# Ring tiles and `ones` moved to the weights' address modulo 512 bytes, and the gate's last tile in two halves of tokens

## The chip, the cores and the metric

The kernel runs on one core of a Trainium2 chip. The metric is the device time of one execution, in microseconds (us). Four compute engines work side by side on tiles of 128 partitions: TensorE (PE in the profile; its weight loads have a row of their own, PEld), VectorE (DVE), ScalarE (ACT) and GpSimd (POOL). SyncE (SP) issues the DMAs. Each engine takes its own instructions in order; semaphores tie the engines together.

On-chip memory (SBUF) is addressed by partition and by byte within the partition. "Modulo 512" below is the byte address of a tile within its partition, modulo 512.

## The reference

One decoder layer over 2,048 tokens of width 1,024: two groups of token mixers (a gated delta rule and HGRN2), an output projection, a squared-ReLU MLP of width 4,096, and a per-layer embedding `p` that is projected, normed and gated by a projection of the residual.

```python
hn = rms_norm(h, pre_mix_norm[i])
proj = jnp.einsum('btd,dc->btc', hn, w_in[i]).astype(f32)
...
mix = jnp.concatenate([o_a.reshape(bsz, t_len, GDN_WIDTH),
                       o_b.reshape(bsz, t_len, HGRN_WIDTH)], axis=-1).astype(h.dtype)
mix_out = jnp.einsum('btc,cd->btd', mix, w_out[i])
h = h + rms_norm(mix_out, post_mix_norm[i])

u = jnp.einsum('btd,df->btf', rms_norm(h, pre_mlp_norm[i]), w_mlp_up[i])
y = jnp.einsum('btf,fd->btd', jnp.square(jax.nn.relu(u)), w_mlp_down[i])
h = h + rms_norm(y, post_mlp_norm[i])

e = rms_norm(jnp.einsum('bte,ed->btd', p[i], w_ple_proj[i]), ple_norm[i])
gate = jax.nn.sigmoid(jnp.einsum('btd,de->bte', h, w_ple_gate[i]))
h = h + e * gate
```

## The kernel before

**Layout.** Activations are held transposed: 128 features on the partitions, tokens along the free dimension. The 2,048 tokens are four blocks `q` of 512 (`QT`), which is the width of one PSUM bank in fp32. A product of 1,024 features takes eight blocks `k` of 128.

**Split operands.** Each fp32 operand of a large product is held as two fp32r tiles, a rounded high part and the rest (`split`, L161 to L164). A product is three matmuls for each block `k`: weight high by data high, weight high by data low, weight low by data high (`product`, L1102). The weights are the stationary operand of 128x128, that is 512 bytes in each partition; the data are the moving operand of 128x512, that is 2,048 bytes in each partition.

**Stages.** PE's order is written out by hand (the manual schedule for PE, L304); SP's order is too in the mixers and from the MLP on. The stages follow each other on PE:

- *Embedding and mixers:* `mme` (the projection of `p`, L190) and `mm` (the input projection, L1031), 192 and 3,168 matmuls of 512 columns (96 of the latter named `mm_ab`). Between the matmuls of `mm` stand the small fp32 matmuls of the mixers, placed by an agenda that counts matmuls (`tick` and `half`).
- *Output projection:* `mmo`, 768 matmuls.
- *MLP,* for two halves of the tokens, each with an up part `u` of 1,344 and a down part `d` of 1,344 matmuls. Both use Strassen's seven products in place of eight, so VectorE makes sums and differences of blocks between them. In the first block of the up part (weights `w_u`) the last five products are interleaved: three matmuls into one bank, then three into the next.
- *Gate:* `mmg`, 768 matmuls, in two halves; in each, for eight output blocks `d`, the two blocks of tokens follow each other. After a product ACT takes a tanh (L1690), DVE does three steps on it (L1691 to L1693), and the result is stored. The stores of a step `d` are kept in `puts` and issued at the start of the next one (L1678), those of the last step at the end (L1698).

**Where tiles lie.** Pools take SBUF in the order in which they are opened, upward from the bottom; `wp` and later `bp` are taken from the top (`side="right"`). A pool's tiles follow each other, and each tile of a ring has a size that is a multiple of 512 bytes, so that all of a ring's tiles share one address modulo 512. The moving tiles of `mm` and `mme` come from the ring `ra` (10 tiles). From the output projection on, `next_pool` hands out moving tiles in turns of 28: ten from `ra`, then 18 from `rb`. `mixT`, `t` and `h2T` are such tiles. In the gate's second half the tiles of block `q` = 2 all lie in `rb`, and those of `q` = 3 all in `ra`. In the down part both operands (`db` moving, `da` stationary) are tiles of one ring, `bp`. The small tiles of the pools `cp` and `sm`, which have odd sizes, decide at which address the rings behind them begin.

The addresses that the build assigns, modulo 512 bytes:

| tiles | used as | before | after |
|---|---|---:|---:|
| `wp`, `bp`: `w`, `w_out`, `wu`, `wg`, `da` | stationary | 480 | 480 |
| `bp`: `db` | moving in `d` | 480 | 480 |
| `ra`: `pT`, `xt`, 10 of 28 turns of `mixT`, `t`, `h2T` | moving | 288 | 480 |
| `rb`: 18 of 28 turns of `mixT`, `t`, `h2T` | moving | 448 | 480 |
| `st`: `hl` (sums of squares in the norms) | moving | 288 | 480 |
| `ones` | stationary with `hl` | 288 | 480 |
| the mixers' own tiles (`m2`, `mp`) | both, small matmuls | 256 | 288 |

The high and low parts of a moving tile lie 2,048 bytes apart and the blocks of a weight tile 512 bytes apart, so these numbers hold for every matmul.

Of the kernel before, what the change touches and what calls it, by code (L numbers as in the profile page):

```python
# [20 lines left out]
P = 128  # L21
T = 2048
D = 1024
KD = D // P
QT = 512
NQ = T // QT
NC = QT // P
# [57 lines left out]
def trunk(ctx, tc, x, xT, pT, vecs, w_in, w_ab, gdn_a_log, gdn_dt_bias, w_out, w_up, w_down,  # L85
          w_ple, w_gate, consts, out):
    nc = tc.nc
    V, S, G, PE = nc.vector, nc.scalar, nc.gpsimd, nc.tensor

    cp = ctx.enter_context(tc.tile_pool(name="cp", bufs=1))  # L90
    ra = ctx.enter_context(tc.tile_pool(name="ra", bufs=10))
    wctx = ctx.enter_context(ExitStack())
    wp = wctx.enter_context(tc.tile_pool(name="wp", bufs=3, side="right"))
    st = ctx.enter_context(tc.tile_pool(name="st", bufs=2))
    sm = ctx.enter_context(tc.tile_pool(name="sm", bufs=3))
    dr = ctx.enter_context(tc.tile_pool(name="dr", bufs=1, space=DRAM))
    pm = ctx.enter_context(tc.tile_pool(name="pm", bufs=2, space=PSUM))
    pp = ctx.enter_context(tc.tile_pool(name="pp", bufs=4, space=PSUM))
# [10 lines left out]
    cm = mixers.enter_context(tc.tile_pool(name="cm", bufs=1))  # L109
    cst = cm.tile([P, N_CONST, P], F32, name="cst")  # L110
    rows = cp.tile([N_ROWS, P], F32, name="rows")
    dec = cp.tile([4, 2], F32, name="dec")
    ident = cst[:, C_IDENT, :]
    negm = cst[:, C_NEG : C_NEG + 2, :]
    unit = cst[:, C_UNIT, :].rearrange("p (g i) -> p g i", i=SB)
    mask = [cst[:, C_MASK + n, : P if n else P // 2] for n in range(len(LEVELS))]

    cols = cp.tile([P, N_ROWS], F32, name="cols")
    ple_w = cp.tile([P, KD], F32, name="ple_w")

    def col(r):
        return cols[:, r : r + 1]


    lg = cols[:, R_LB : R_LB + 4]
    lb = cp.tile([P, 4], F32, name="lb")
    lb1 = cp.tile([P, 4], F32, name="lb1")
    ha = cp.tile([P, 4], F32, name="ha")
    hna = cp.tile([P, 4], F32, name="hna")
    hb = cp.tile([P, 4], F32, name="hb")  # L130
    nexpa = cp.tile([4, 1], F32, name="nexpa")

    def vectors():

# [12 lines left out]
        S.activation(nexpa, dec[:, 0:1], AF.Exp)  # L147
        V.tensor_scalar(nexpa, nexpa, -1.0, None, ALU.mult)

    mhalf = cp.tile([P, NC], F32, name="mhalf")  # L150
    V.memset(mhalf, -0.5)
    one = cm.tile([P, P], F32, name="one")
    ones = cp.tile([P, P], F32R, name="ones")
    V.memset(one, 1.0)
    V.tensor_copy(ones, one)

# [91 lines left out]
    def tok(q):  # L248
        return slice(q * QT, (q + 1) * QT)
# [64 lines left out]
    xin = {}  # L314
# [42 lines left out]
    with ExitStack() as ectx:  # L357
        es = ectx.enter_context(tc.tile_pool(name="es", bufs=1))
        with tc.manual_schedule(engines={mybir.EngineType.SP}):
            ple0 = stage_ple(0, "plea0")  # L360
            praw = [es.tile([P, 2, QT], F32, name=f"praw{q}") for q in range(2)]
            nc.sync.dma_start(praw[0], pT[:, tok(0)].rearrange("(k p) t -> p k t", p=P))
            rows4 = x[tok(0), :].rearrange("(p c) d -> p c d", c=NC)
            xs = es.tile([P, NC, D], F32, name="xs")
            for c in range(0, NC, 2):
                nc.sync.dma_start(xs[:, c : c + 2], rows4[:, c : c + 2])
            nc.sync.dma_start(ident, consts[:, C_IDENT])
            nc.sync.dma_start(rows, vecs)
            nc.sync.dma_start(dec[:, 0:1], gdn_a_log.rearrange("o h -> h o"))
            nc.sync.dma_start(dec[:, 1:2], gdn_dt_bias.rearrange("o h -> h o"))  # L370
            nc.sync.dma_start(praw[1], pT[:, tok(1)].rearrange("(k p) t -> p k t", p=P))
            ple1 = stage_ple(1, "plea1")
            xraw = es.tile([P, KD, QT], F32, name="xraw")
            for k in range(0, KD, 2):
                nc.sync.dma_start(xraw[:, k : k + 2],
                                  xT[k * P : (k + 2) * P, tok(0)].rearrange("(k p) t -> p k t", p=P))
            nc.sync.dma_start(cst[:, C_NEG:], consts[:, C_NEG:])

            ple = [ple0(V), None]
            pts = [[operand(ra, None, f"pT{q}_{k}", raw=praw[q][:, k]) for k in range(2)] for q in range(1)]  # L380
            ss = sm.tile([P, NC], F32, tag="ss", name="ss_x0")
            for c in range(NC):
                S.activation(xs[:, c], xs[:, c], AF.Square, accum_out=ss[:, c : c + 1])
            V.tensor_scalar(ss, ss, 1.0 / D, EPS, ALU.mult, ALU.add)
            rsqrt(ss)
            stores = []
            for d in range(4):
                stores.append(embed_tile(0, d, ple[0], pts[0], accs, es, 6))
                if d == 1:
                    vectors()  # L390
            pts.append([operand(ra, None, f"pT1_{k}", raw=praw[1][:, k]) for k in range(2)])
            ple[1] = ple1(V)
# [12 lines left out]
    with mixers as mctx:  # L405
# [23 lines left out]
        def x_scale(q):  # L429
            ss2 = sm.tile([P, 2, NC], F32, tag="ss2", name=f"ss2_x{q}")  # L430
            rows4 = x[tok(q), :].rearrange("(p c) d -> p c d", c=NC)
            halves, loaded = [(c, a) for c in range(NC) for a in range(2)], []
            for i in range(len(halves) + 1):
                if i < len(halves):
                    c, a = halves[i]
                    t = m2.tile([P, QT], F32, tag="ld", name=f"xs{q}_{c}_{a}", bufs=2)
                    nc.sync.dma_start(t, rows4[:, c, a * QT : (a + 1) * QT])
                    loaded.append(t)
                if i:
                    c, a = halves[i - 1]  # L440
                    t = loaded.pop(0)
                    S.activation(t, t, AF.Square, accum_out=ss2[:, a, c : c + 1])
                yield
            ss = sm.tile([P, NC], F32, tag="ss", name=f"ss_x{q}")
            V.tensor_tensor(ss, ss2[:, 0, :], ss2[:, 1, :], ALU.add)
            V.tensor_scalar(ss, ss, 1.0 / D, EPS, ALU.mult, ALU.add)
            rsqrt(ss)
            yield
            x_r[q] = spread(ss, f"x{q}")
# [828 lines left out]
    prep, x = None, {}  # L1278
# [391 lines left out]
    for half in range(2):  # L1670
        qs = (2 * half, 2 * half + 1)
        if half == 0:
            later(gate_operands(2), range(8, 24, 2))
            later(gate_operands(3), range(32, 48, 2))
        for d in range(KD):
            w = gated.pop((half, d))
            for a in puts:
                nc.sync.dma_start(*a)  # L1678
            puts = []
            if d + 1 == KD and half == 0:  # L1680
                rsb = {q: spread_load(ple_r[q], f"pg{q}", None, "acc", 3) for q in (2, 3)}
            for s, q in enumerate(qs):
                ps = bank(f"mmg_{q}_{d}", pp)
                product(ps, columns(*w), xin[q])
                nq, nd = (q, d + 1) if d + 1 < KD else (q + 2, 0)
                if nq < NQ:
                    es[nq, nd] = embedded(nq, nd, rsb[nq])
                t = es.pop((q, d))
                e, th = t[:, 0], t[:, 1]
                S.activation(th, ps, AF.Tanh, scale=0.5)  # L1690
                V.scalar_tensor_tensor(th, th, 1.0, e, ALU.add, ALU.mult)  # L1691
                V.tensor_tensor(th, th, xin[q][d][:, 0, :], ALU.add)
                V.tensor_tensor(th, th, xin[q][d][:, 1, :], ALU.add)  # L1693
                puts.append((out[blk(d), tok(q)], th))
                if s == 0:
                    gate_weights(half, d + 2)
    for a in puts:
# [46 lines left out]
```

## Time and profile before

| what | us |
|---|---:|
| time, median of 3 runs | 2778.44 |
| lowest and highest of the 3 | 2771.64 and 2778.57 |
| the profiled execution: its span, first to last instruction | 2778.2 |
| PE busy in it | 2696.7 |
| DVE busy | 2048.2 |
| ACT busy | 1471.2 |

The page lists the span of the profiled execution and no further time of its own; the span is 0.2 us below the median of the runs. "Busy" is the union of an engine's instructions. A matmul's row gives the mean length of one from start to end (about 390 to 400 ns), but matmuls overlap: what counts is how far one starts after the other, and that is a stretch of PE's work divided by its count.

The stages on PE, by the first start and the last end of their matmuls in the trace: `mme` and `mm` 7 to 1140 us, `mmo` 1141 to 1337, the first `u` 1336 to about 1662, the first `d` until about 1982, the second `u` until 2286, the second `d` until 2594, `mmg` until 2772.

### The profile page before, as it was taken

The numbers are of one execution on the slowest core, as the hardware profiler recorded it, in microseconds if no ns is written. First come the engines' busy times: TensorE is split into PE (matmuls) and PEld (weight loads), VectorE is DVE, ScalarE is ACT, GpSimd is POOL, SyncE is SP. The second block draws the span as 40 slices with busy tenths as digits, with TensorE's granted clock in tenths as the row PEclk, the third lists the DMA queues.
The fourth block names the chain that finished last, engine by engine and source line by source line (L and its number), as shares of the span: only waits on it lengthen the run. The fifth ranks groups of instructions, "written<-read, shape, count | busy, mean of one in ns | idle before, by whom it ended". The sixth has DMA issues, their size and how long they took to land.

```text
span 2778.2 us, 38362 instructions
## 1 busy us (share of the span) xinstructions
PE 2696.7 (97%) x12721; PEld 2219.1 (80%) x12721; DVE 2048.2 (74%) x4242; ACT 1471.2 (53%) x2943; POOL 104.2 (4%) x104
## 2 busy tenths in 40 slices
PE   7999999999999999999899999999999999999999
PEld 5787788878888887777688887887888888887887
DVE  6787877787787777578889867758787765567775
ACT  6665554455545445676555545545454455465431
POOL 0000000000000000000000000001000000001000
PEclk9999999999999999999999999999999999999999
DMA  7776776667666665887466547667454446577663
GB/s 261 261 242 217 230 249 220 218 215 244 231 211 215 213 213 166 267 300 241 141 222 217 181 149 252 222 192 247 155 197 145 147 165 210 190 254 246 213 207 118
DMA packets 268598, 589.24 MB, mean 212 GB/s; under 512 B 55642, under 2 KB 59960, under 8 KB 249200
## 3 DMA queue, kind: packets, MB, share of 16 engines
q1 hardware_dynamic: 268400, 586.79, 63.2%
q8 instruction: 101, 1.65, 0.2%
q14 instruction: 97, 0.79, 0.1%
HBM read 419.75 MB, written 166.92 MB: 211 GB/s over the span
## 4 chain that ended last, share of the span: by engine, by line
PE 62%; DVE 9%; DMA 8%; issue 6%; ACT 3%; SPq 1%; POOL 1%; DVEq 0%; POOLq 0%; ACTq 0%
PE u L1100 22%; PE d L1100 20%; PE mm L1031 9%; PE mmg L1100 6%; DMA ud_g<-u_g 2%; DMA sys_g<-ud_g 1%; DVE pr_g L667 1%; DVE xs_g L670 1%; DVE xs_g L672 1%; PE mmo L1100 1%; DMA mixT<-mixd 1%; DMA rsb_g<-rd_g 1%; DMA b<-h1d 0%; DMA rd_g<-m_g 0%; DVE acc_vg L511 0%
## 5 line engine op out<-in xcount | busy, mean ns | idle before, releaser
L1031 PE MATMUL mm<-xt,w 128*128 128x512 f32 x3072 | 787.0, 403 | 1.9 <-ACT qk_h L767 0.9
L1031 PEld LDWEIGHTS mm<-xt,w 128*128 128x128 f32 x3072 | 558.6, 190 | 109.7 <-ACT qk_h L767 1.3
L1100 PE MATMUL d<-db,da 128*128 128x512 f32 x2688 | 613.0, 390 | 3.9 <-DVE db L217 1.9
L1100 PE MATMUL u<-t,wu 128*128 128x512 f32 x2604 | 608.0, 396 | 3.3 <-ACT wu L163 3.3
L1100 PEld LDWEIGHTS d<-db,da 128*128 128x128 f32 x2688 | 503.9, 188 | 112.3 <-DVE db L217 4.7
L1100 PEld LDWEIGHTS u<-t,wu 128*128 128x128 f32 x2604 | 489.5, 188 | 121.2 <-ACT wu L163 4.1
L217 DVE TENSOR_TENSOR db<-db 128x512 fp32r<-128x512 f32 x224 | 161.2, 720 | 72.6 <-ACT db L216 71.7
L1429 DVE TENSOR_TENSOR u<-u,u 128x512 f32<-128x512 f32 x224 | 150.3, 682 | 72.5 <-PE u L1100 71.3
L216 ACT ACTIVATE db<-db 128x512 fp32r<-128x512 f32 x224 | 140.9, 629 | 82.2 <-DMA db<-hid 80.2
L1100 PE MATMUL mmo<-mixT,w_out 128*128 128x512 f32 x720 | 172.9, 401 | 7.2 <-DVE w_out L164 5.8
L1100 PE MATMUL mmg<-h2T,wg 128*128 128x512 f32 x768 | 178.1, 394 | 0.0
L1470 ACT ACTIVATE u<-u 128x512 f32<-128x512 f32 x128 | 81.0, 633 | 179.5 <-DVE u L1429 179.0
L1100 PEld LDWEIGHTS mmg<-h2T,wg 128*128 128x128 f32 x768 | 144.3, 188 | 33.5
L1100 PEld LDWEIGHTS mmo<-mixT,w_out 128*128 128x128 f32 x720 | 137.3, 191 | 41.8 <-DVE w_out L164 7.1
L164 DVE TENSOR_TENSOR da<-da 128x512 fp32r<-128x512 f32 x128 | 92.7, 724 | 90.2 <-ACT da L163 89.8
L163 ACT ACTIVATE da<-da 128x512 fp32r<-128x512 f32 x128 | 80.5, 629 | 137.6 <-DMA da<-sumd 113.0
L163 ACT ACTIVATE wu<-a 128x512 fp32r<-128x512 f32 x124 | 74.1, 624 | 47.9 <-DMA a<-in_w_up_dram 45.1
L667 DVE TENSOR_TENSOR pr_g<-xs_g,sys_g 128x16 f32<-128x16 f32 (+14 forms) x240 | 93.8, 391 | 5.4
L227 POOL TENSOR_TENSOR acc_y<-acc_y,sq_y 128x512 f32<-128x512 f32 x28 | 38.4, 1371 | 1393.3 <-ACT sq_y L226 1393.3
L164 DVE TENSOR_TENSOR wu<-a,wu 128x512 fp32r<-128x512 f32 x124 | 84.7, 686 | 4.9 <-ACT wu L163 4.8
L1471 ACT ACTIVATE u<-u 128x512 f32<-128x512 f32 x128 | 80.8, 631 | 3.7
L672 DVE SCALAR_TENSOR_TENSOR xs_g<-xs_g,sys_g 128x4 f32<-128x4 f32 x256 | 57.6, 225 | 29.3 <-DMA sys_g<-ud_g 23.9
(374 smaller groups left out, 3817.6 us busy)
## 6 DMA issues: line engine op xcount, KB each, us to landing
w<-cache_in SPq DMA_DIRECT2D x96, 1024.0 KB
db<-hid SPq DMA_DIRECT2D x224, 256.0 KB
cache_in<-w SPq DMA_DIRECT2D x32, 1024.0 KB
hid<-u SPq DMA_DIRECT2D x128, 256.0 KB
da<-sumd SPq DMA_DIRECT2D x128, 256.0 KB
a<-in_w_up_dram SPq DMA_DIRECT2D x124, 256.0 KB
hid<-ht SPq DMA_DIRECT2D x96, 256.0 KB
dr<-in_w_down_dram SPq DMA_DIRECT2D x96, 256.0 KB
```

What stands on the lines that cost most here:

```text
L163: S.activation(t[:, 0], raw, AF.Copy)
L164: eng.tensor_tensor(t[:, 1], raw, t[:, 0], ALU.subtract)
L216: S.activation(t[:, 0], plain(t), AF.Copy)
L217: V.tensor_tensor(t[:, 1], plain(t), t[:, 0], ALU.subtract)
L227: eng.tensor_tensor(acc, acc, sq, ALU.add)
L667: V.tensor_tensor(pr[:, :, :, 0:i], xs[:, None, :, 0:i].broadcast_to([P, 2, GC, i]), sys[:, 0:i, i : i + 2].rearrange("p j two -> p two j" ...
L672: V.scalar_tensor_tensor(xs[:, :, i + 1], xs[:, :, i], sys[:, i, i + 1 : i + 2], xs[:, :, i + 1], ALU.mult, ALU.add)
L1031: PE.matmul(ps, *terms[i], start=i == 0, stop=i == nt - 1)
L1100: PE.matmul(ps, a, b, start=start, stop=stop)
L1429: V.tensor_tensor(c[new], c[old], ps, ALU.add)
L1470: S.activation(c[k], c[k], AF.Relu)
L1471: S.activation(c[k], c[k], AF.Square)
```

## The change

It does two things.

**Addresses.** Small tiles go into a new pool `c0` ahead of the ring `ra`; `cp` is opened behind `st`, with `ones` as its first tile; a pad of 64 bytes goes into `sm`. With that, `ra`, `st`, `ones` and `rb` begin at 480 modulo 512, as the table shows. The column of scales `ss_x` moves to `c0` with two buffers where it had three.

**The last tile.** For the last block of tokens and the last output block (`q` = 3, `d` = 7) the product is done for the first 256 tokens into one bank and then for the other 256 into a second one; tanh, the three steps on DVE and the store are done for each half.

```diff
-    cp = ctx.enter_context(tc.tile_pool(name="cp", bufs=1))
+    c0 = ctx.enter_context(tc.tile_pool(name="c0", bufs=1))
     ra = ctx.enter_context(tc.tile_pool(name="ra", bufs=10))
     wctx = ctx.enter_context(ExitStack())
     wp = wctx.enter_context(tc.tile_pool(name="wp", bufs=3, side="right"))
     st = ctx.enter_context(tc.tile_pool(name="st", bufs=2))
+    cp = ctx.enter_context(tc.tile_pool(name="cp", bufs=1))
+    ones = cp.tile([P, P], F32R, name="ones")
     sm = ctx.enter_context(tc.tile_pool(name="sm", bufs=3))
+    sm.tile([P, 16], F32, tag="pad", name="pad", bufs=1)
...
-    dec = cp.tile([4, 2], F32, name="dec")
+    dec = c0.tile([4, 2], F32, name="dec")
...
-    ple_w = cp.tile([P, KD], F32, name="ple_w")
+    ple_w = c0.tile([P, KD], F32, name="ple_w")
...
-    lb = cp.tile([P, 4], F32, name="lb")
+    lb = c0.tile([P, 4], F32, name="lb")
...
-    ones = cp.tile([P, P], F32R, name="ones")
...
-            ss = sm.tile([P, NC], F32, tag="ss", name="ss_x0")
+            ss = c0.tile([P, NC], F32, tag="ss", name="ss_x0", bufs=2)
...
             for s, q in enumerate(qs):
-                ps = bank(f"mmg_{q}_{d}", pp)
-                product(ps, columns(*w), xin[q])
+                parts = [slice(0, QT)] if (q, d) != (NQ - 1, KD - 1) else [slice(0, QT // 2), slice(QT // 2, QT)]
+                banks = []
+                for i, at in enumerate(parts):
+                    ps = bank(f"mmg_{q}_{d}_{i}", pp)[:, : at.stop - at.start]
+                    product(ps, columns(*w), [x[:, :, at] for x in xin[q]])
+                    banks.append((at, ps))
...
-                e, th = t[:, 0], t[:, 1]
-                S.activation(th, ps, AF.Tanh, scale=0.5)
-                V.scalar_tensor_tensor(th, th, 1.0, e, ALU.add, ALU.mult)
-                V.tensor_tensor(th, th, xin[q][d][:, 0, :], ALU.add)
-                V.tensor_tensor(th, th, xin[q][d][:, 1, :], ALU.add)
-                puts.append((out[blk(d), tok(q)], th))
+                for at, ps in banks:
+                    e, th = t[:, 0, at], t[:, 1, at]
+                    S.activation(th, ps, AF.Tanh, scale=0.5)
+                    V.scalar_tensor_tensor(th, th, 1.0, e, ALU.add, ALU.mult)
+                    V.tensor_tensor(th, th, xin[q][d][:, 0, at], ALU.add)
+                    V.tensor_tensor(th, th, xin[q][d][:, 1, at], ALU.add)
+                    puts.append((out[blk(d), q * QT + at.start : q * QT + at.stop], th))
```

The order of the instructions on every engine is the same as before up to the last tile of the gate. At the program's end, PE's rows of the last product were these (`mmg` is the bank, `h2T` the moving tiles, `wg` the weights; the size is that of the output):

```order
L1100 MATMUL mmg_7_25963<-h2T_0_25165,wg_7_0_25826 128x512 x3
L1100 MATMUL mmg_7_25963<-h2T_1_25203,wg_7_0_25826 128x512 x3
L1100 MATMUL mmg_7_25963<-h2T_2_25233,wg_7_0_25826 128x512 x3
L1100 MATMUL mmg_7_25963<-h2T_3_25253,wg_7_0_25826 128x512 x3
L1100 MATMUL mmg_7_25963<-h2T_4_25291,wg_7_1_25831 128x512 x3
L1100 MATMUL mmg_7_25963<-h2T_5_25325,wg_7_1_25831 128x512 x3
L1100 MATMUL mmg_7_25963<-h2T_6_25345,wg_7_1_25831 128x512 x3
L1100 MATMUL mmg_7_25963<-h2T_7_25383,wg_7_1_25831 128x512 x3
```

Now there are twice as many of half the width, in two banks; around the turn from the first bank to the second they read:

```order
L1102 MATMUL mmg_7_0_25967<-h2T_5_25329,wg_7_1_25835 128x256 x3
L1102 MATMUL mmg_7_0_25967<-h2T_6_25349,wg_7_1_25835 128x256 x3
L1102 MATMUL mmg_7_0_25967<-h2T_7_25387,wg_7_1_25835 128x256 x3
L1102 MATMUL mmg_7_1_25992<-h2T_0_25169,wg_7_0_25830 128x256 x3
L1102 MATMUL mmg_7_1_25992<-h2T_1_25207,wg_7_0_25830 128x256 x3
L1102 MATMUL mmg_7_1_25992<-h2T_2_25237,wg_7_0_25830 128x256 x3
```

So each weight block is loaded six times in this product where it was loaded three times. On DVE the end of the program was, with `eg` the tile of the embedding and the tanh:

```order
L1691 SCALAR_TENSOR_TENSOR eg_7_25893<-eg_7_25893 128x512
L1692 TENSOR_TENSOR eg_7_25893<-eg_7_25893,h2T_7_25042 128x512
L1693 TENSOR_TENSOR eg_7_25893<-eg_7_25893,h2T_7_25042 128x512
L1691 SCALAR_TENSOR_TENSOR eg_7_25925<-eg_7_25925 128x512
L1692 TENSOR_TENSOR eg_7_25925<-eg_7_25925,h2T_7_25383 128x512
L1693 TENSOR_TENSOR eg_7_25925<-eg_7_25925,h2T_7_25383 128x512
```

and is now:

```order
L1698 SCALAR_TENSOR_TENSOR eg_7_25897<-eg_7_25897 128x512
L1699 TENSOR_TENSOR eg_7_25897<-eg_7_25897,h2T_7_25046 128x512
L1700 TENSOR_TENSOR eg_7_25897<-eg_7_25897,h2T_7_25046 128x512
L1698 SCALAR_TENSOR_TENSOR eg_7_25929<-eg_7_25929 128x256
L1699 TENSOR_TENSOR eg_7_25929<-eg_7_25929,h2T_7_25387 128x256
L1700 TENSOR_TENSOR eg_7_25929<-eg_7_25929,h2T_7_25387 128x256
L1698 SCALAR_TENSOR_TENSOR eg_7_25929<-eg_7_25929 128x256
L1699 TENSOR_TENSOR eg_7_25929<-eg_7_25929,h2T_7_25387 128x256
L1700 TENSOR_TENSOR eg_7_25929<-eg_7_25929,h2T_7_25387 128x256
```

The last three steps were one triple of 512 tokens and became two triples of 256. ACT has one tanh more and SP one store more, in the same manner.

More of the change, by code (lines that the diff above doesn't have):

```diff
@@ L125, in trunk @@
     lg = cols[:, R_LB : R_LB + 4]
-    lb = cp.tile([P, 4], F32, name="lb")
[L127 to L131, printed above, removed]
+    lb = c0.tile([P, 4], F32, name="lb")
+    lb1 = c0.tile([P, 4], F32, name="lb1")
+    ha = c0.tile([P, 4], F32, name="ha")
+    hna = c0.tile([P, 4], F32, name="hna")
+    hb = c0.tile([P, 4], F32, name="hb")
+    nexpa = c0.tile([4, 1], F32, name="nexpa")
     def vectors():
@@ L148, in vectors @@
         V.tensor_scalar(nexpa, nexpa, -1.0, None, ALU.mult)
-    mhalf = cp.tile([P, NC], F32, name="mhalf")
+    mhalf = c0.tile([P, NC], F32, name="mhalf")
     V.memset(mhalf, -0.5)
     one = cm.tile([P, P], F32, name="one")
-    ones = cp.tile([P, P], F32R, name="ones")
     V.memset(one, 1.0)
@@ L443, in x_scale @@
                 yield
-            ss = sm.tile([P, NC], F32, tag="ss", name=f"ss_x{q}")
+            ss = c0.tile([P, NC], F32, tag="ss", name=f"ss_x{q}", bufs=2)
             V.tensor_tensor(ss, ss2[:, 0, :], ss2[:, 1, :], ALU.add)
```

## The prediction

> **What bounds the kernel now.** I read the page from the top: the span, the engines, the chain that ended last and its shares.
>
> ```profile
> span 2778.2 us, 38362 instructions
> PE 2696.7 (97%) x12721; PEld 2219.1 (80%) x12721; DVE 2048.2 (74%) x4242; ACT 1471.2 (53%) x2943; POOL 104.2 (4%) x104
> PE 62%; DVE 9%; DMA 8%; issue 6%; ACT 3%; SPq 1%; POOL 1%; DVEq 0%; POOLq 0%; ACTq 0%
> PE u L1100 22%; PE d L1100 20%; PE mm L1031 9%; PE mmg L1100 6%; DMA ud_g<-u_g 2%; DMA sys_g<-ud_g 1%; DVE pr_g L667 1%; DVE xs_g L670 1%; DVE xs_g L672 1%; PE mmo L1100 1%; DMA mixT<-mixd 1%; DMA rsb_g<-rd_g 1%; DMA b<-h1d 0%; DMA rd_g<-m_g 0%; DVE acc_vg L511 0%
> ```
>
> PE is busy 97% of the span. The chain runs through it in the up part `u`, the down part `d` and the gate `mmg`, and only for a small part in the mixers (`mm`) and the output projection (`mmo`). The change takes no large matmul away, so the question is how far apart matmuls start. The groups give counts and the idle time before them (the last numbers):
>
> ```profile
> L1031 PE MATMUL mm<-xt,w 128*128 128x512 f32 x3072 | 787.0, 403 | 1.9 <-ACT qk_h L767 0.9
> L1100 PE MATMUL d<-db,da 128*128 128x512 f32 x2688 | 613.0, 390 | 3.9 <-DVE db L217 1.9
> L1100 PE MATMUL u<-t,wu 128*128 128x512 f32 x2604 | 608.0, 396 | 3.3 <-ACT wu L163 3.3
> L1100 PE MATMUL mmo<-mixT,w_out 128*128 128x512 f32 x720 | 172.9, 401 | 7.2 <-DVE w_out L164 5.8
> L1100 PE MATMUL mmg<-h2T,wg 128*128 128x512 f32 x768 | 178.1, 394 | 0.0
> ```
>
> All five have the same shapes, yet `d` takes 613.0/2688 = 228 ns for each matmul and `u` 608.0/2604 = 233 ns. The chain in order of time (start, length, what) has long unbroken runs, which give cleaner rates:
>
> ```profile
> 1552.46 107.30 PE u L1100 x460
> 1683.61 193.21 PE d L1100 x851
> 1982.61 303.23 PE u L1100 x1304
> 2299.92 212.61 PE d L1100 x938
> 2603.47 168.56 PE mmg L1100 x728
> ```
>
> That is 233.3, 227.0, 232.5, 226.7 and 231.5 ns. Only in `d` do moving and stationary tiles share their address modulo 512 (480 and 480); in `u` and `mmg` the moving tiles are at 448 or 288. So before already holds both cases. Two rows more rule out the nearest other reasons. `d` turns to another bank after every three matmuls, and so does most of the first block of `u`, which the timeline shows (start, length, count):
>
> ```profile
> 1353.00 10.41 PE L1100 MATMUL u<-t,w_u 128*128 128x512 f32 x44
> ```
>
> Less the 0.40 us that the last one takes, 10.0/43 = 233 ns: turning banks doesn't make a product fast. And the gate's last products differ in the ring alone. The tanh on ACT starts when a product is done:
>
> ```profile
> 2760.95 0.60 ACT L1690 ACTIVATE eg<-mmg 128x512 f32<-128x512 f32 x1 [4.90 <-PE mmg L1100]
> 2766.61 0.60 ACT L1690 ACTIVATE eg<-mmg 128x512 f32<-128x512 f32 x1 [5.07 <-PE mmg L1100]
> 2772.11 0.60 ACT L1690 ACTIVATE eg<-mmg 128x512 f32<-128x512 f32 x1 [4.90 <-PE mmg L1100]
> ```
>
> The 24 matmuls of `q` = 2 (`rb`, 448) took 5.66 us, the 24 of `q` = 3 (`ra`, 288) 5.50 us: same weights, same code, 236 against 229 ns.
>
> The Trainium skill says otherwise: by SBUF — State Buffer, section "Who interferes with whom", PE reads moving data and weights through two independent ports and never waits on anyone. By that rule no address would matter and the change would be worth its tail alone; it is the first rival below. These rows disagree with it.
>
> **The change, part by part.** After it all large matmuls stand as those of `d` do. I take 226.8 ns for them, between the two runs of `d`.
>
> *Up part.* The first block (84 matmuls) lies among waits, so I leave it out; it could add 0.5 us. The first half then has 1260 x (233.3 - 226.8) = 8.2 us, the second 1344 x (232.5 - 226.8) = 7.7 us. What could take the place of PE is DVE, which makes the weights' sums. The windows (PE, PEld, DVE, ACT, POOL busy, clock, DMA) of the two halves:
>
> ```profile
> 1372.00:1660.00 288.00, 287.19 (x1230) 231.51 (x1231) 233.94 (x378) 158.37 (x264) 0.00 (x0) 1.00 0.56 193
> 1983.00:2285.00 302.00, 302.00 (x1301) 244.12 (x1300) 224.61 (x357) 154.34 (x255) 0.00 (x0) 1.00 0.47 161
> ```
>
> DVE works 233.94 of 288 us (81%); against a stage shorter by 8.2 us that is 84%. PE waits for nothing there. I take all of it: **15.9 us**.
>
> *Gate.* 744 x (231.5 - 226.8) = **3.5 us**; PE has no idle time in its row.
>
> *Mixers.* The rate of `mm` from an unbroken run of the chain, and what the chain and the waits say of the stage:
>
> ```profile
> 668.11 3.68 PE mm L1031 x16
> by line: PE mm L1031 28.8%; issue 13.2%; DMA ud_g<-u_g 4.9%; DMA sys_g<-ud_g 4.0%; DVE pr_g L667 3.7%; DVE xs_g L670 2.7%; DVE xs_g L672 2.3%; DMA rsb_g<-rd_g 1.7%; DVE acc_vg L511 1.4%; DVE raw_xt L952 1.3%; DVE xt L164 1.2%; SPq L647 1.2%
> PE psc_g L743 <- ACT w_g L740: 14.4, 15, 4.1
> 100.00:600.00 500.00, 477.62 (x2566) 402.91 (x2565) 391.45 (x1098) 275.85 (x692) 25.39 (x29) 0.99 0.70 230
> 600.00:1100.00 500.00, 492.99 (x2701) 419.63 (x2699) 381.53 (x1117) 259.39 (x688) 27.86 (x32) 1.00 0.64 215
> ```
>
> 3.68/16 = 230.0 ns, so 3.2 ns are to be had 3360 times (`mm`, `mm_ab`, `mme`): 10.8 us. But between 262 and 1140 us the chain spends only 28.8% in `mm`; it goes through round trips of DMA and short DVE steps, and PE waits for the recurrence (`psc_g`) in 15 places. There a faster PE waits longer. On the other side PE is busy 477.62 and 492.99 of 500 us, and much of what those waits hang on was itself released by PE some tens of us earlier. So between 29% (3.1 us) and all (10.8 us); nearer the lower middle: **6.0 us**. The mixers' small matmuls move both operands together from 256 to 288 and keep their distance; I cost that at nothing, and the norms' matmuls, equal at 288 before and at 480 after, too.
>
> *Output projection.* Its moving tiles are split over the rings as the gate's are, so 768 x 4.7 = 3.6 us are to be had. But its chain is elsewhere:
>
> ```profile
> by line: issue 19.0%; PE mmo L1100 9.9%; DMA b<-h1d 6.2%; DVE w_out L164 5.1%; DMA mixT<-mixd 5.0%; DVE t L164 4.0%; DVE acc_o L227 3.1%; ACT L1137 2.9%; DMA raw_out<-in_w_out_dram 2.7%; ACT L1136 2.5%; DVE yo L1170 2.5%; ACT w_out L163 2.4
> ```
>
> 9.9% of it would give 0.4, all of it 3.6; I take **1.0 us**.
>
> *The last tile.* After the last matmul come one tanh, three DVE steps and a store, one behind the other. Rows of before for the full and the half width, for narrow matmuls, and for the store's issue:
>
> ```profile
> 2772.11 0.60 ACT eg L1690
> 2772.74 0.70 DVE eg L1691
> L767 ACT ACTIVATE th_h<-mm x32: 363/381/383, 89.8 to 1067.7; 128x256 f32<-128x256 f32 x32
> L635 DVE TENSOR_TENSOR y_kg<-y_kg,gf_g 128x256 f32<-128x256 f32 x16 | 6.6, 414 | 0.0
> 467.56 0.45 PE at_h L822 x4
> 2774.91 0.33 SPq L1698 DMA_DIRECT2D out_dram<-eg  x1
> ```
>
> For the second half the tanh takes 0.38 in place of 0.60 and each DVE step 0.41 in place of 0.70: 0.22 + 3 x 0.29 = 1.1 us less behind the last matmul. The first half's steps (0.38 + 3 x 0.41 = 1.6 us) lie under the second bank's product. The store runs from 2774.91 to the span's end, 3.3 us, and now carries half the bytes: between 0 and half of that, I take 0.3. Matmuls of 256 columns in this format aren't in the trace. Below, half of 226.8 or the 0.45/4 = 112 ns of narrow matmuls that each load their own weights: 48 x 113 = 5.4 us against 5.5 before. Above, the weight load sets the pace and a half takes as long as a whole: 48 x 226.8 = 10.9 us. The narrow row is the nearest, so 0.1 us less. Sum **1.5 us**, with ends at 4.0 lost and 2.8 gained.
>
> *The rest.* `ss_x` with two buffers: each is used once per block of tokens, hundreds of us apart, so nothing waits.
>
> Sum: 15.9 + 3.5 + 6.0 + 1.0 + 1.5 = 27.9 us. Span 2778.2 - 27.9 = 2750.3; the median lies 0.2 above the span: **2750.5 us**.
>
> **Rivals.**
> *The address is not the reason* (6%). Then `d` is faster because its two operands come from one ring, or were written just before use, and only the tail is left: 2778.4 - 1.5 = 2777. For it: no other stage has equal addresses in a long run. Against it: 233 ns with turning banks, and 236 against 229 ns for two rings in one code.
>
> *Another engine takes over* (6%). If DVE, at 81%, holds the first half of `u`, and mixers and output projection give nothing, 8.2 + 6.0 + 1.0 are lost: 2766. Against it: no wait for DVE in `u` behind its first block.
>
> *The clock falls where PE waits* (3%), the one that ends slower. In the mixers one wait of 4 us was followed by slow matmuls (timeline, then windows with the clock behind POOL):
>
> ```profile
> 431.09 0.80 PE L743 MATMUL psc_g<-w_g,kt_g 128*128 128x128 f32 x2 [4.06 <-ACT w_g L740]
> 433.67 3.31 PE L1031 MATMUL mm<-xt,w 128*128 128x512 f32 x8
> 424.00:432.00 8.00, 3.94 (x22) 3.21 (x21) 7.31 (x28) 5.42 (x14) 0.00 (x0) 0.84 1.02 387
> 432.00:440.00 8.00, 8.00 (x39) 7.02 (x39) 6.81 (x22) 1.60 (x3) 1.01 (x1) 0.73 0.48 172
> ```
>
> Eight matmuls took 3.31 us, 414 ns each, and at clocks of 0.84 and 0.73 the 16 us lost 8 x 0.16 + 8 x 0.27 = 3.4 us. If all 15 waits at `psc_g` grew to 4 us, that would cost 15 x 3.4 = 51 us: 2802. It decides from a wait of about 4 us on; but a head's share of `mm`, some 200 matmuls, saves 0.6 us, and the mean wait is 14.4/15 = 1.0 us. The Trainium skill gives the same point in TensorE: Matmul & The Clock Gate, Part 1 (half rate after an idle window of about 3.4 us); the wait of 4.06 us agrees.
>
> **How the numbers follow.** The forecast has 85%. Its low end takes everything: 15.9 + 0.5 + 3.5 + 10.8 + 3.6 + 2.8 = 37.1, so 2741; runs of before also lie up to 6.8 us under their median, so 2738. Its high end takes 3.1 from the mixers, nothing from the output projection and the dear tail: 15.9 + 3.5 + 3.1 - 4.0 = 18.5, so 2760; a part of the second rival brings 2763. A difference of 0.3% (8.3 us) is about what a measurement of this kernel can tell. Forecast and second rival are faster by more (90%), the first lies within (7%), the third is slower (3%).
>
> **What would show it.** In the profile after: runs of `u` and `mmg` on the chain at 226 to 228 ns for each matmul, `u` and `mmg` as fast as `d`, and `d` unchanged; `mm` at 227 in unbroken runs, with `psc_g` waits grown by a few us in total; behind the last matmul one tanh of 0.38 and three steps of 0.41 us. The prediction is wrong if `u` stays at 233 ns, if a wait for DVE appears in `u`, or if the matmuls of 256 columns start over 200 ns apart.

## The result, and the profile after

The changed kernel takes 2758.36 us (median of 4 runs, 2755.88 to 2764.09) against 2777.82 us for the one before (4 runs, 2771.64 to 2778.57). The ratio is **0.993**, with a 95% interval of 0.991 to 0.994: 19.5 us faster, where 27.9 were forecast. The profiled execution took 2759.13 us, 1.8 us more than its span.

From the page of the changed kernel: the span, the busy times, and the five groups of large matmuls (count, then busy time and mean ns of one, then idle time of PE ahead of them):

```profile
span 2757.3 us, 38414 instructions
PE 2673.0 (97%) x12745; PEld 2221.0 (81%) x12745; DVE 2046.0 (74%) x4245; ACT 1469.8 (53%) x2944; POOL 104.2 (4%) x104
L1033 PE MATMUL mm<-xt,w 128*128 128x512 f32 x3072 | 785.5, 402 | 1.3 <-ACT zt_zg L548 0.7
L1102 PE MATMUL d<-db,da 128*128 128x512 f32 x2688 | 613.5, 390 | 5.8 <-DVE db L219 3.2
L1102 PE MATMUL u<-t,wu 128*128 128x512 f32 x2604 | 593.3, 390 | 3.5 <-ACT wu L165 3.4
L1102 PE MATMUL mmo<-mixT,w_out 128*128 128x512 f32 x720 | 170.5, 398 | 9.7 <-DVE w_out L166 6.2
L1102 PE MATMUL mmg<-h2T,wg 128*128 128x512 f32 (+1 forms) x792 | 174.7, 383 | 0.0
```

PE has 24 instructions more (the halves) and is busy 23.7 us less; the other engines do what they did. `u` lost 14.7 us, `d` nothing, and `mm`, which has the most matmuls, only 1.5 us. The unbroken runs on the chain that ended last (start, length) give the rates:

```profile
1368.60 80.69 PE u L1102 x348
1449.75 94.29 PE u L1102 x416
1544.49 104.28 PE u L1102 x460
1673.28 207.69 PE d L1102 x915
1972.87 295.60 PE u L1102 x1304
2587.03 165.36 PE mmg L1102 x752
```

The second `u` run went from 232.5 to 295.60/1304 = 226.7 ns for each matmul, the rate of `d` (207.69/915 = 227.0). Of the first half's runs two are as fast (94.29/416 and 104.28/460 = 226.7), the first is not: 80.69/348 = 231.9.

The weight loads are not what became shorter. Their group in `u`, before and then after, has the same length, 188 ns for each load; what fell, by 14.7 us, is the idle time between the loads:

```profile
L1100 PEld LDWEIGHTS u<-t,wu 128*128 128x128 f32 x2604 | 489.5, 188 | 121.2 <-ACT wu L163 4.1 <-DVE wu L164 0.9
L1102 PEld LDWEIGHTS u<-t,wu 128*128 128x128 f32 x2604 | 489.6, 188 | 106.5 <-ACT wu L165 4.2 <-DVE wu L166 0.7
```

Cut at the first matmul of each stage, the two executions compare so (lengths taken before rounding):

| stage | starts, before | starts, after | length before | after | difference |
|---|---:|---:|---:|---:|---:|
| work ahead of `mm_ab` | 0 | 0 | 44.8 | 45.3 | +0.5 |
| mixers | 44.8 | 45.3 | 1096.1 | 1090.8 | -5.2 |
| `mmo` | 1140.8 | 1136.2 | 195.6 | 195.6 | 0.0 |
| first `u` | 1336.4 | 1331.7 | 326.0 | 319.6 | -6.4 |
| first `d` | 1662.4 | 1651.3 | 310.0 | 311.3 | +1.3 |
| second `u` | 1972.4 | 1962.6 | 313.3 | 305.7 | -7.6 |
| second `d` | 2285.7 | 2268.3 | 307.9 | 308.8 | +0.9 |
| `mmg` | 2593.5 | 2577.1 | 178.5 | 175.3 | -3.2 |
| behind the last matmul | 2772.0 | 2752.4 | 6.1 | 4.9 | -1.2 |
| span | | | 2778.2 | 2757.3 | -20.9 |

The output projection is the stage in which PE became faster and nothing was won. Its windows, before and then after (length, then busy time of PE, PEld, DVE, ACT, POOL with counts, granted clock, DMA share, GB/s):

```profile
1140.84:1336.43 195.59, 188.21 (x799) 150.63 (x798) 142.08 (x211) 122.81 (x192) 3.02 (x3) 0.98 0.79 265
```

```profile
1136.16:1331.73 195.57, 185.87 (x800) 151.52 (x798) 141.99 (x211) 122.28 (x192) 3.02 (x3) 0.97 0.78 265
```

PE is busy 2.3 us less in a stage of the same length: the time turned into waiting, as the group's idle time says too (7.2 before, 9.7 now, most of it for `w_out`). The end of the program on ACT (tanh, with PE's product ahead of it in brackets) and on DVE:

```profile
2741.22 0.60 ACT L1697 ACTIVATE eg<-mmg 128x512 f32<-128x512 f32 x1 [4.84 <-PE mmg L1102]
2746.72 0.60 ACT L1697 ACTIVATE eg<-mmg 128x512 f32<-128x512 f32 x1 [4.90 <-PE mmg L1102]
2749.59 0.39 ACT L1697 ACTIVATE eg<-mmg 128x256 f32<-128x256 f32 x1 [2.27 <-PE mmg L1102]
2752.41 0.38 ACT L1697 ACTIVATE eg<-mmg 128x256 f32<-128x256 f32 x1 [2.43 <-PE mmg L1102]
...
2752.82 0.43 DVE L1698 SCALAR_TENSOR_TENSOR eg<-eg 128x256 f32<-128x256 f32 x1 [1.47 <-ACT eg L1697]
2753.28 0.43 DVE L1699 TENSOR_TENSOR eg<-eg,h2T 128x256 f32<-128x256 f32 x1
2753.74 0.42 DVE L1700 TENSOR_TENSOR eg<-eg,h2T 128x256 f32<-128x256 f32 x1
```

The halves' products ended 2.87 and 2.82 us after the tanh ahead of them, so the 48 matmuls of 256 columns start (2.87 + 2.82)/48 = 119 ns apart.

### The profile page after: what moved, and what is told of

Same layout as the page of the kernel before. It is cut to its first block, busy times and chain, and to the rows that moved or that the text cites. A ratio compares the mean times of both kernels' runs of the same rounds, so it can differ in the third digit from the quotient of the medians.

```text
span 2757.3 us, 38414 instructions
## 1 busy us (share of the span) xinstructions
PE 2673.0 (97%) x12745; PEld 2221.0 (81%) x12745; DVE 2046.0 (74%) x4245; ACT 1469.8 (53%) x2944; POOL 104.2 (4%) x104
## 4 chain that ended last, share of the span: by engine, by line
PE 63%; DVE 10%; DMA 8%; issue 5%; ACT 4%; SPq 1%; POOL 1%; DVEq 0%; POOLq 0%; ACTq 0%
PE u L1102 21%; PE d L1102 19%; PE mm L1033 11%; PE mmg L1102 6%; DMA ud_g<-u_g 1%; DMA sys_g<-ud_g 1%; PE mmo L1102 1%; DVE pr_g L669 1%; DVE xs_g L672 1%; DMA raw_out<-in_w_out_dram 1%; DVE xs_g L674 1%; DVE raw_xt L954 1%; DMA db<-hid 1%; DVE xt L166 1%; DMA b<-h1d 1%
## 5 line engine op out<-in xcount | busy, mean ns | idle before, releaser
L1102 PE MATMUL u<-t,wu 128*128 128x512 f32 x2604 | 593.3, 390 | 3.5 <-ACT wu L165 3.4
L1102 PE MATMUL mmg<-h2T,wg 128*128 128x512 f32 (+1 forms) x792 | 174.7, 383 | 0.0
L166 DVE TENSOR_TENSOR da<-dr,da 128x512 fp32r<-128x512 f32 x96 | 66.3, 690 | 17.6 <-ACT da L165 15.4
```

Source lines behind the costliest of these rows:

```text
L166: eng.tensor_tensor(t[:, 1], raw, t[:, 0], ALU.subtract)
L1102: PE.matmul(ps, a, b, start=start, stop=stop)
```

## The experiments

What was forecast is the address theory: a large matmul starts 226.7 ns after the one before it where its two operands have the same address modulo 512, and 4 to 7 ns later otherwise. Three questions were put: is it the address, and of which ring; what is the period and how does the price depend on the distance; and why did the mixers not become as fast.

### 1 and 2: the two halves of the change, each alone

Addresses alone, the changed kernel without the halves:

```diff
-                parts = [slice(0, QT)] if (q, d) != (NQ - 1, KD - 1) else [slice(0, QT // 2), slice(QT // 2, QT)]
+                parts = [slice(0, QT)]
```

> The addresses of the change, the gate's last tile whole as before. Theory (the equal address modulo 512 gives nearly all of the gain): 2758.4 + 1.2 = about 2760 us, u and mmg at 226 to 227 ns for each matmul. Rival (the last tile in halves matters): clearly above 2765.

Measured: 2760.83 us (2758.49 to 2765.39), ratio 0.994 [0.992, 0.995]. The second `u` run took 295.58 us for its 1304 matmuls, as after.

The halves alone, in the kernel before:

```diff
-                ps = bank(f"mmg_{q}_{d}", pp)
-                product(ps, columns(*w), xin[q])
+                parts = [slice(0, QT)] if (q, d) != (NQ - 1, KD - 1) else [slice(0, QT // 2), slice(QT // 2, QT)]
+                banks = []
+                for i, at in enumerate(parts):
...
```

> The addresses of before, the gate's last tile in two halves. Theory: only the tail changes, some 1.2 us less than before (2777.8): 2776 to 2777, and on the chain u stays at 232 to 234 ns, mmg at 231 to 232. The mixers end where they ended before (the first mmo starts at 1140.8 us), within a us. Rival (the mixers' end wanders from build to build by some us whatever the addresses): the first mmo starts 3 us or more away from 1140.8.

Measured: 2778.18 us (2776.56 to 2782.11), ratio 1.000 [0.999, 1.001]. `u` ran as before (303.23/1304 = 232.5 ns), and behind the last matmul stood 4.9 us in place of 6.1. So the gain belongs to the addresses. The tail's 1.2 us are seen in the trace but not in the time, whose interval of 0.1% either way (2.8 us) is wider than that. One thing missed the theory and nearly reached the rival's 3 us: although nothing changed ahead of the gate, the mixers ended 2.8 us earlier than before. The first block of `mmo` in this run (count, lengths, from when to when):

```profile
L1059 PE MATMUL mmo<-mixT,w_out x48: 388/392/481, 1138.0 to 1151.1; 128*128 128x512 f32 x48
```

Before, it began at 1140.8, after the change at 1136.2. The mixers' length moves by itself; experiment 5 comes back to it.

### 3: one ring at a time

`rb` alone to 480 (`ra` stays at 288), in the kernel before:

```diff
+    sm.tile([P, 8], F32, tag="pad", name="pad", bufs=1)
```

> Before with 32 bytes of padding, so that the ring rb lies at 480 as the weights do and ra stays at 288; last tile whole. rb holds 64% of u's and 56% of mmg's and mmo's moving tiles. Theory: u saves 1728 x 6.7 = 11.6, mmg 432 x 6.7 = 2.9, the mixers nothing: about 2763; the last products of the gate take 5.44 us for q = 2 and still 5.50 for q = 3. Rival (the relation of both rings matters): less than half of that, above 2770.

Measured: 2771.09 us (2766.37 to 2778.51), ratio 0.998 [0.997, 0.999]. The gain is 6.8 us, under half of the change's.

`ra` alone at 480 (`rb` back at 448), in the changed kernel:

```diff
-    sm.tile([P, 16], F32, tag="pad", name="pad", bufs=1)
+    sm.tile([P, 8], F32, tag="pad", name="pad", bufs=1)
```

> After with 32 bytes less of padding: ra and the norms' tiles at 480, rb at 448; last tile in halves. Theory: u saves 960 x 5 = 4.7, mmg 336 x 2.3 = 0.8, the mixers the 4.7 us that they gained in after, the tail 1.2: about 2766. If the mixers' gain is not of the addresses: about 2771, with the first mmo starting near 1140.

Measured: 2774.82 us (2772.55 to 2778.97), ratio 0.999 [0.998, 1.000], a gain of 3.1 us. Both theories missed, and on the same side; with `rb` alone it was the rival's number that came (above 2770). Together they are 6.8 + 3.1 = 9.9 us, with 1.2 us of tail in the second, where both rings together brought 2777.88 - 2760.83 = 17.1 us. **The gains don't add up.** The chain's `u` runs of the two kernels, `rb` alone and then `ra` alone:

```profile
1976.33 300.92 PE u L1101 x1304
```

```profile
1976.60 303.02 PE u L1102 x1304
```

`u` takes 18 of 28 tiles from `rb` and 10 from `ra`, that is 864 and 480 of 1344 matmuls. The steady prices of the addresses of before are 6.6 ns for a tile of `rb` and 2.2 ns for one of `ra` (the table of experiment 4). If each matmul paid for its own tile alone, `rb` in place would have given 864 x 6.6 ns = 5.7 us; the run went from 303.23 to 300.92 us, 2.3 less. `ra` in place should have given 480 x 2.2 ns = 1.1 us and gave 0.2. By the starts of `u`'s matmuls in the trace, those with a tile of `rb` began 230.7 ns after the one ahead of them though they now had the weights' address. The gate, where a whole product takes its tiles from one ring, shows why. With `rb` alone at 480, a product of `rb` follows one of `ra`, and the gaps in it were, by the same starts:

```
behind the 1st to 10th matmul of the product:   224 to 236 ns, up and down
behind the 11th to 24th:                        226.8 ns
```

So a matmul at another address costs not only itself; up to ten matmuls behind it still run unevenly. In `u` the rings change after three to nine matmuls nearly everywhere, and one misplaced ring spoils most of the other's gain. One place in each block of the second `u` has 18 matmuls of `rb` in a row, and there the gaps came to 226.6 to 226.8 ns from the eleventh on. The products of the gate in this run, by the tanh behind each:

```profile
2751.52 0.60 ACT L1691 ACTIVATE eg<-mmg 128x512 f32<-128x512 f32 x1 [4.91 <-PE mmg L1101]
2757.07 0.60 ACT L1691 ACTIVATE eg<-mmg 128x512 f32<-128x512 f32 x1 [4.95 <-PE mmg L1101]
2762.59 0.60 ACT L1691 ACTIVATE eg<-mmg 128x512 f32<-128x512 f32 x1 [4.92 <-PE mmg L1101]
```

The product of `rb` took 5.55 us (5.66 before the change), that of `ra` 5.52 us. The starts of the matmuls are the finer measure (a median over the products of the gate's second half): 5.49 us for `rb` (5.61 before), not the 24 x 226.7 ns = 5.44 of an even run, and 5.51 us for `ra` (5.49 before).

### 4: the distance and the period

Three kernels put the rings at other distances from the weights, by a first tile `shift` in `c0`, the pad in `sm`, and `gcol` taken from `sm` to the mixers' pool `mp`:

```diff
+    c0.tile([P, 64], F32, name="shift")
...
-    sm.tile([P, 16], F32, tag="pad", name="pad", bufs=1)
+    sm.tile([P, 120], F32, tag="pad", name="pad", bufs=1)
...
-            gcol = sm.tile([P, NC, 36], F32, tag="gcol", name=f"gcol_{q}", bufs=2)
+            gcol = mp.tile([P, NC, 36], F32, tag="gcol", name=f"gcol_{q}", bufs=2)
```

This one has `ra` 256 bytes and `rb` 32 bytes away from the weights; `shift` of 16 columns with the old pad gives 64 and -64, 32 columns with a pad of 112 give 128 and -128.

> After with ra 256 bytes and rb 32 bytes above the weights' address modulo 512 (gcol moved to the mixers' pool to make room). Theory (period 512, any distance costs): the last products of the gate take 5.50 to 5.70 us for q = 2 (rb) and, for q = 3 (ra), 24 matmuls at 229 ns or more; u at 230 to 235 ns on the chain. Rival (the period is 256 or less): ra's products stay at 226.7 ns, 5.44 us.

> After with ra 64 bytes above and rb 64 bytes below the weights' address modulo 512. Theory: neither ring is at 226.7 ns; rb between the 233.8 of 32 bytes below and the 229 to 232 of 192 below. Rival (only some distances collide, or the sign decides): one ring at 226.7 ns.

> After with ra 128 bytes above and rb 128 bytes below the weights' address modulo 512. Theory: neither ring at 226.7 ns. Rival (a period of 128): both at 226.7.

Measured in one execution each: 2778.87, 2771.56 and 2782.68 us, beside 2779.62 us for the kernel before (median of 7 runs). The gate's products in the kernel with 256 and 32:

```profile
2755.27 0.60 ACT L1698 ACTIVATE eg<-mmg 128x512 f32<-128x512 f32 x1 [5.00 <-PE mmg L1103]
2760.75 0.60 ACT L1698 ACTIVATE eg<-mmg 128x512 f32<-128x512 f32 x1 [4.88 <-PE mmg L1103]
2766.41 0.60 ACT L1698 ACTIVATE eg<-mmg 128x512 f32<-128x512 f32 x1 [5.07 <-PE mmg L1103]
```

The product of `ra`, 256 bytes away, took 5.48 us, that of `rb`, 32 bytes away, 5.66 us (5.60 by the starts). Behind the first ten matmuls of a product the steady gaps were these, with the distances of the kernels before and after among them (0, -32 and -192):

| distance, modulo 256 | seen at | ns for each large matmul |
|---:|---|---:|
| 0 | 0; 256 | 226.7 |
| 32 | +32 | 233.3 |
| 64 | +64; -192 | 228.9 |
| 128 | +128; -128 | 232.4 |
| 192 | -64 | 233.3 |
| 224 | -32 | 233.3 |

Two distances 256 apart (+64 and -192) have the same rate, with the same pattern of gaps (226.2, 228.9, 231.6). So with 64 and 128 bytes the theory's side came true (neither ring at 226.7 ns), with 256 bytes the rival's, in the steady gaps. The table speaks for a period of 256 bytes and against 512. The fourth kernel is the test: the changed one with `ra` moved to 224, 256 bytes away from the weights, and `rb` left at 480.

```diff
+    c0.tile([P, 64], F32, name="shift")
...
-    sm.tile([P, 16], F32, tag="pad", name="pad", bufs=1)
+    sm.tile([P, 112], F32, tag="pad", name="pad", bufs=1)
...
-            gcol = sm.tile([P, NC, 36], F32, tag="gcol", name=f"gcol_{q}", bufs=2)
+            gcol = mp.tile([P, NC, 36], F32, tag="gcol", name=f"gcol_{q}", bufs=2)
```

> After with ra (and the norms' tiles) 256 bytes away from the weights' address modulo 512 and rb at it. Theory A (period 512, as the change has it): ra's matmuls are slow and spoil those of rb behind them, as in the kernel with rb alone: 2768 to 2772, u at 230 to 232 ns on the chain. Theory B (the period is 256; in the kernel with distances 256 and 32 ra's matmuls came to 226.7 ns from about the eighth on): u and mmg at 226.7 ns as in after, 2757 to 2762.

Measured: 2762.66 us (2757.36 to 2765.27), ratio 0.994 [0.992, 0.996] to 2780.26 us for the one before. Its chain:

```profile
1370.18 79.43 PE u L1103 x348
1450.07 94.29 PE u L1103 x416
1544.82 104.28 PE u L1103 x460
1972.11 295.59 PE u L1103 x1304
2585.26 165.36 PE mmg L1103 x752
```

All as in the changed kernel, to 0.01 us, but for the first run. **For matmuls of 512 columns the period is 256 bytes.** That all moving tiles are alike is not enough: at 128 and -128 they are alike too, modulo 256, and take 232.4 ns. One thing stays open. The weights lay at 480 in every kernel, so "the distance to the weights" and "the moving tile's own address" (best at 224 modulo 256) can't be told apart by these runs. For the distance there is only an argument: 224 is no round address, while the moving tile at 0 modulo 256 (a distance of 32) is among the slowest.

The first run, 79.43 us against 80.69 after, answers another question: why these 348 matmuls gained so little. Windows over their start, after the change and then in this kernel (clock third from the end):

```profile
1368.00:1396.00 28.00, 27.40 (x114) 22.50 (x115) 27.20 (x45) 18.98 (x33) 0.00 (x0) 0.94 0.72 240
```

```profile
1368.00:1396.00 28.00, 25.82 (x113) 21.09 (x114) 27.86 (x47) 18.61 (x33) 0.00 (x0) 1.00 0.73 244
```

In the profiled execution after the change the granted clock was 0.94 for 28 us behind the waits for `w_u` and `wu`; at full clock the run is 1.26 us shorter. The kernel with addresses alone shows 1.00 and 79.45 us there as well.

### 5: the mixers

`mm` kept its rate: over the steady steps from one large matmul to the next (512 columns, the first behind a small one left out, under 400 ns) the starts give 230.1 ns before (2664 steps, 613.1 us) and 229.7 after (2663 steps, 611.7 us), not 227. An unbroken run of 16, which took 3.68 us before, takes 3.66, that is 228.8 ns for each matmul:

```profile
454.84 3.66 PE mm L1033 x16
```

The first idea was that the mixers' small tiles, 192 bytes away from the weights, are to blame. They were put at 480, in the changed kernel:

```diff
+        mp.tile([P, 48], F32, name="shift")
```

> After with 192 bytes of padding in the mixers' pool, so that the mixers' own tiles lie at 480 too. In after mm still took 229.7 ns on average between the mixers' small matmuls though moving tiles and weights share 480. Theory (the first matmuls behind a group of small ones are slow whatever the addresses): mm stays at 229 to 230 ns and the time within 0.15% of after. Rival (the small tiles' other address is what costs there): mm near 227 ns, some 2700 x 2.7 = 7 us less PE time in the mixers, and 2 to 6 us less in the whole.

Measured: 2759.38 us (2757.96 to 2763.75), ratio 0.993 [0.991, 0.994], like the change itself. `mm` stayed at 229.7 ns, and its group is where it was:

```profile
L1034 PE MATMUL mm<-xt,w 128*128 128x512 f32 x3072 | 783.8, 401 | 4.5 <-DVE acc_vg L514 2.5
```

So the small tiles' address is not it. The other idea was that a small matmul as such disturbs the large ones behind it, whatever its address. The mean gaps of `mm` by position behind the last small matmul, after the change, fit that (from the starts in the trace):

```
position  0     1      2      3      4      5      6      7      8      9      10 and on
ns        315   230.4  232.8  233.9  227.0  231.1  232.0  227.4  229.1  228.3  226.7 to 227.0
```

From the tenth on the theory's rate is there; before the change those positions had 228 to 231 ns. To see it without the mixers, one small fp32 matmul was added ahead of each of the gate's 32 products, which otherwise run without a gap. Its operands, a block of `h2T` and `ones`, both lie at 480, and its bank is read by nobody:

```diff
+                small = bank(f"small_{q}_{d}")
+                PE.matmul(small[:, :P], ones.bitcast(F32), plain(xin[q][0])[:, :P], start=True, stop=True)
```

> After with one small fp32 matmul (128x128 by 128 columns, as the mixers' are, its result unused) ahead of each of the gate's 32 products. Theory (a small matmul breaks the even run, and the some ten large ones behind it are slow, which is why mm in the mixers gained so little): starts behind it 228 to 234 ns apart for eight to ten matmuls, then 226.7; a product of 24 takes 5.44 + 0.11 + 0.04 = 5.59 us. Rival (a small matmul costs its own 0.11 us alone): 5.55 us, and 226.7 ns from the second large matmul on.

Measured: 2770.12 us in one execution; the gate took 183.6 us against 175.3, that is 8.2 us before rounding, or 0.26 us for each small matmul. PE's timeline in it:

```profile
2620.12 0.38 PE L1688 MATMUL small<-h2T,ones 128*128 128x128 f32 x2
2620.25 5.74 PE L1102 MATMUL mmg<-h2T,wg 128*128 128x512 f32 x24
2625.83 0.38 PE L1688 MATMUL small<-h2T,ones 128*128 128x128 f32 x2
2625.97 5.74 PE L1102 MATMUL mmg<-h2T,wg 128*128 128x512 f32 x24
```

From one small matmul to the next are 5.71 us, where 24 even ones take 5.44 us. The small one itself (two records) takes 0.13 us, from 2620.12 to 2620.25; the other 0.13 us are lost in the large matmuls behind it. Their median gaps are 314, 235, 233, 236, 224, 231, 236, 228, 232.5 and 231 ns, and 227 from then on: the mixers' pattern, and from the third gap on also the one behind the other ring in experiment 3 (233, 236, 224, 231, 236, 228, 233, 230). The direction is the theory's, the price larger than it said. Its 0.04 us for the uneven gaps were right (0.05); what it had left out is the first gap, 314 ns in place of 227.

What then of the 5.2 us by which the mixers were shorter? Where they ended, by the first `mmo` matmul, in three more builds: 1138.0 us with the addresses of before (experiment 2),

```profile
L1062 PE MATMUL mmo<-mixT,w_out x48: 388/392/481, 1135.4 to 1149.2; 128*128 128x512 f32 x48
```

1135.4 with the rings at 64 and -64, earlier than with equal addresses, but

```profile
L1062 PE MATMUL mmo<-mixT,w_out x48: 387/393/477, 1141.9 to 1155.0; 128*128 128x512 f32 x48
```

1141.9 with both rings and the small tiles at 480. Over all twelve builds the mixers' length lies between 1090.2 and 1096.1 us, in no order of the addresses. The profiled difference of 5.2 us is inside that wander. (Each build was profiled once, so whether it belongs to the build or to the single execution is open; 25 executions of the kernel before lie between 2774.49 and 2783.47 us.) What the addresses saved of `mm`'s work is 613.1 - 611.7 = 1.4 us, and some 1.1 us in the steps from a large to a small matmul.

## Why the prediction was right, and where not

**The mechanism** was right: the address decides, `u` and `mmg` came to the rate of `d`, and `d` stayed. The first rival (the address is not the reason, 2777 us) is out by experiments 1 and 2: the same code at other addresses gains 17 us, the halves alone gain nothing. The reason given with it was off in three ways that the large terms did not need: the period is 256 bytes, not 512; a misplaced matmul costs up to ten behind it as well, so that both rings had to be moved; and equal addresses are not best for matmuls of 256 columns (the last tile, below). The 236 and 229 ns read from the gate's tanhs are 233.6 and 228.8 by the starts of the matmuls; the difference between the rings is real, but smaller than it looked. The rule of the Trainium skill weighed there (SBUF — State Buffer, "Who interferes with whom": PE reads moving data and weights through independent ports) gives no difference between these kernels; 303.23 against 295.60 us for the same 1304 matmuls say that there is one. What in PE or the memory makes it was not tried; the weight loads take 188 ns either way.

**Up part**, 15.9 forecast, 14.0 measured. The terms 1344 x 5.7 ns = 7.7 us (measured 7.6) and the first half's were right in kind. The first half gave 6.4 where 8.2 were forecast; 1.26 us of what is missing went with a clock of 0.94 in the profiled execution. With the clock at 1.00 (experiment 4) the halves gave 326.0 - 318.1 = 7.9 and 7.6, 15.5 in all. No wait for DVE came up, so the second rival is out.

**Gate**, 3.5 forecast, 3.2 measured.

**Mixers**: here the prediction went wrong. Its step was "3.2 ns are to be had 3360 times (`mm`, `mm_ab`, `mme`): 10.8 us", of which 6.0 were taken. The 230.0 ns of an unbroken run of 16 matmuls were read as the price of the address. They were mostly the trail of the small matmul ahead of that run, which remains: `mm` went from 230.1 to 229.7 ns, the run of 16 from 3.68 to 3.66 us, and after the change the same steps are still 611.7 - 2663 x 0.2267 = 8.0 us above an even run. To be had were about 2.5 us (1.4 + 1.1 above), not 10.8, before any question of what the chain passes on. The profiled 5.2 us look like a hit on the forecast's 6.0, but that is luck: they lie inside the mixers' own wander, and the medians leave little room for them, as `u`, gate and tail are 18.4 of the 19.5 us.

**Output projection**, 1.0 forecast, 0.0 measured: PE's 2.3 us became waiting. By the chain, the stage hangs on its weights' way through DMA and DVE, with 9.9% in `mmo`. Whether those 9.9% (0.4 us) were there can't be told: over the twelve builds the stage takes 194.3 to 198.8 us.

**The last tile**, 1.5 forecast, 1.2 measured behind the last matmul. The tanh took 0.38 as forecast, the DVE steps 0.43 in place of 0.41, so 0.22 + 0.27 x 3 = 1.0 us, and 0.2 came from the store. The two halves' products took 5.69 us, 0.25 longer than one full product; 0.1 shorter was forecast, with 113 ns for a matmul of 256 columns where 119 were measured. The 113 ns were right for the addresses of before. In experiment 2, with `ra` at 288, the tanh ahead of the two halves starts at 2765.80, and theirs are these:

```profile
2768.52 0.38 ACT L1695 ACTIVATE eg<-mmg 128x256 f32<-128x256 f32 x1 [2.12 <-PE mmg L1100]
2771.18 0.38 ACT L1695 ACTIVATE eg<-mmg 128x256 f32<-128x256 f32 x1 [2.28 <-PE mmg L1100]
```

That is 5.38 us for the two products, and 113.3 ns from one of their matmuls to the next by the starts. At 480 the same matmuls start 119.9 ns apart, and 256 bytes away from it 119.9 and 120.0 (experiment 4); at 64 bytes it is 117.8, at 128 bytes 118.6. So the first part of the change made the second one dearer: equal addresses, the best case for 512 columns, are the worst one seen for 256.

**The clock rival** did not come about: the waits at `psc_g` are 14.9 us in 13 places (the longest 4.5), against 14.4 in 15.

```profile
PE psc_g L745 <- ACT w_g L742: 14.9, 13, 4.5
```

A small form of it did, the 28 us at a clock of 0.94 in one execution.

**The sum.** Of the 27.9 us forecast, 20.9 are in the span. By stages the forecast lost 1.9 in `u`, 0.3 in the gate, 1.0 in `mmo`, 0.3 at the end, and 2.2 in the down parts, which were left alone (their lengths differ by 2 to 3 us from build to build: 309.3 to 312.5 and 307.2 to 309.0); the mixers count 4.7 by their end where 6.0 were taken. Besides, the 0.2 us between span and time were wrong: the execution's own time is 1.8 us above its span. And at the range's low end the working gives 2741 - 6.8 = 2734, where 2738 was written; nothing hangs on it here.

## What to carry to other kernels

Where the same matmul has two rates in one profile, sort its rows by the operands' addresses: here, placing all moving tiles at the weights' address modulo 256 was worth 2.5% of an unbroken stretch of `u` and 1.8% of the gate, without moving an instruction. This was seen for matmuls of 512 columns, with the weights at one address; for 256 columns the same place was the slowest of those tried, so measure the width that you use. Move all rings that alternate in a stretch, since one left behind keeps the others slow. Take the gain from long unbroken runs alone; where other matmuls break in every ten or so, hardly any of it is to be had, and where PE waits for a transfer anyway, none.

## What the runs showed of the hardware

- The time from one 128x512 fp32r matmul with a weight load of its own to the next depends on the address of its moving tile modulo 256 bytes. With the weights at 480 modulo 512 throughout, and counted as the distance from them: 226.7 ns at 0, 228.9 at 64, 232.4 at 128, 233.3 at 32, 192 and 224. The weight loads took 188 ns each, before as after.
- With 256 columns the order is another: 113.3 ns at a distance of -192 bytes, 117.8 at 64, 118.6 at 128, 119.9 at 0, 119.9 and 120.0 at 256, each from the 48 matmuls of one product in a profile. Here -192 and 64 differ, so the period of 256 is not seen.
- A disturbance has a trail of up to ten matmuls. Behind a small fp32 matmul of 0.13 us the next ten large ones lost another 0.13 us together, 0.09 of it in the first gap and the rest in a fixed pattern (235, 233, 236, 224, 231, 236 ns and so on), at the best of addresses. Behind the other ring at a bad address the trail was ten, seven and five gaps long in three builds (`rb` alone, `ra` at 256 with `rb` at 32, `ra` alone); the shorter ones read like the end of the longest (from its sixth gap on 231, 236, 228, 233, 230 ns; the whole of the shortest 230, 236, 228, 232, 231). Why it lasts so long is open.
- The mixers' length varies by 6 us among builds whose work is the same, one profile each, which is as much as any term of this change but one.
